# One grid for all slots, and another order of work at the entry of both FFNs of a hybrid mLSTM and attention trunk

## The chip, the cores and the metric

The kernel runs on one core of one Trainium2 chip. The metric is the device time of one execution in microseconds: the median of three runs of the kernel before is 2521.12 us (2517.9 to 2522.45). All times below are of the kernel before.

## The reference

Input x is 1024 rows of 1024 float32 numbers. Two layers follow one another; each adds a mixer and an FFN to the residual stream, with a norm before and after each (rmsnorm of rows of 1024). Layer 0's mixer is a chunkwise mLSTM with 8 heads, layer 1's a causal attention with forget gates and 16 heads on keys and values that are projected once. What matters here is the FFN, which stands in both layers:

```python
def conv_ffn(h, w_up, conv_w, conv_b, w_down):      # h 1024x1024, w_up 1024x5632
    u = h @ w_up
    up = jnp.pad(u, ((0, 0), (CONV_WIDTH - 1, 0), (0, 0)))
    y = conv_b
    for j in range(CONV_WIDTH):                       # 3 taps along the rows
        y = y + conv_w[j] * up[:, j:j + S]
    gate, val = jnp.split(y, 2, axis=-1)              # 2816 columns each
    return (jax.nn.gelu(gate, approximate=True) * val) @ w_down
```

## The kernel before

**Products.** Every float32 operand of a large product is split into a high and a low part (`split`, L197: ScalarE casts the high part, L199, VectorE subtracts it, L200), and each product is three matmuls: high with high, high with low, low with high. The up product works on column tiles of 128 columns of the gate half and the same 128 of the value half: 22 column tiles in each FFN. A column tile is a 2x2 block product by Strassen and Winograd: seven products named 11, 12, S2, S1, S3, S4 and 22, in that order, each of 12 matmuls of 128x512 (L815), so 84 matmuls for a column tile. Products 11 and 12 run after one another into two banks of PSUM, and so on; a tile's results are copied or added out of the banks by ScalarE (L824) and VectorE (L822). After S4 the value half goes through the convolution of three taps (L831, L833), after 22 the gate half and the Gelu (L848); every second column tile `keep` (L857) forms sums on GpSimd and sends seven pieces to DRAM. The down product (L976) reads them back, in matmuls of the same shape with both operands in the tile x.

**Weights of a column tile.** SyncE loads the raw weights of a tile into slots 8 and 9 (even tiles) or 10 and 11 (odd). `prep_up` makes the stationary operands: 11 goes to slot 18, 12 to slot 0, S2 and S1 (from sums that GpSimd forms in a slot `tmp`, L789 to L792) to slots 1 and 2, S3 and 22 to slots 3 and 4, S4 to slot 5. In the steady state a product of tile f is followed by `prep_up` of the same product of tile f+1, into the same slots.

**The moving operand.** The rows of the normalised residual stream, transposed and split, are the moving operand. Products 11, 12, S3 and 22 read them from x (a tile of 16384 numbers per partition); S2, S1 and S4 read sums of row tiles from the pair slots p0 to p5.

**Slots.** The arena is a set of slots, each one tag of a tile pool with 128 partitions: 1024 numbers wide (4096 bytes), 1088 for slots 0, 1, 15, 27, 29 and 30 (4352 bytes), 1032 for slots 2 and 31 (4128 bytes), and 2048 for p0, p3, p2, p4, p1 and p5 (two slots each, 8192 bytes). They lie behind one another in memory in the order 10, 5, p1, 16, 15, 0, 27, 29, 1, 30, 11, 31, then 8, 18, p0, 7, 3, p3, 6, p4, p2, 4, 2, then 14, p5, 9, 32; x and the identity stand in a second pool. Since 4096, 4352 and 8192 are multiples of 128 and 4128 is 32 more than one, the slots of the second group begin 32 bytes further on a 128-byte line than the first group, and those of the third 64 bytes further. x begins where the third group begins.

**The entry of an FFN.** `out_stage` computes the mixer's output product for eight row tiles, adds it to the residual stream (`tail_a`: Square, scale, L215, L216), normalises the result (`tail_b`, L225), forms sums of two row tiles (`sums`, L730 to L733) and transposes each piece on TensorE with a split into x or a pair slot (`turns`: four transposes of L207, one cast L199, one subtraction L200 a turn). TensorE's instructions stand in source order there (`in_order`). For the last row tiles, `lead` begins the column tiles: products 11 and 12 of tiles 0 and 1, then product 11 of tile 2 with the turns of the last row tile in between, then product 12 of tile 2; `run` goes on with the other five products of tile 0, of tile 1, of tile 2, and then tile after tile. ScalarE and VectorE are ordered by the scheduler.

Of the kernel before, what the change touches and what calls it, by code (L numbers as in the profile page):

```python
# [34 lines left out]
SLACK = 0, 20  # L35
PIECES = {5: (8, 20, 26, 32, 38), 10: (6, 8, 17, 21, 25, 29, 33, 37, 41, 45)}

WIDE = {0: 1088, 1: 1088, 15: 1088, 27: 1088, 29: 1088, 30: 1088, 2: 1032, 31: 1032}
PAIRS = (19, 22), (20, 21), (23, 24), (25, 12), (26, 13), (28, 17)
PAIR = {i: (j, n) for j, two in enumerate(PAIRS) for n, i in enumerate(two)}  # L40
BLOCK = {(0, 0): 0, (0, 1): 1, (1, 1): 2, (1, 0): 3}
# [1 line left out]
ORDER = (0, 4, 1, 5, 2, 6, 3, 7)  # L43
# [5 lines left out]
PRODUCTS = ("11", "12", "S2", "S1", "S3", "S4", "22")  # L49


class Core:
# [30 lines left out]
    def slot(self, i, dt):  # L83
# [3 lines left out]
        if self.slots.get(key, (None, None))[1] != dt:  # L87
            n, name = (WIDE.get(i, 1024), key) if half is None else (2048, f"p{key}")
            self.slots[key] = self.arena.tile([P, n], dt, tag=name, name=name), dt
# [258 lines left out]
def mlstm(k, x, gpre, w_in, b_gate, hnorm, w_out, gpost, gnext, scr, x1, params, follow):  # L348
# [338 lines left out]
    with k.in_order():  # L687
        out_stage(arena, w, None, x, x1, gpost, gnext, follow, ((), (4, 5), (2, 3)), turns=late)


class Ffn:
# [34 lines left out]
    def sums(self, h0, h1):  # L726

        tt = self.nc.vector.tensor_tensor
        (s1, s2), (s3, s4) = ((self.k.f(i)[:, :512], self.k.f(i)[:, 512:]) for i in (31, 27))
        tt(s1, h1[:, :512], h1[:, 512:], ALU.add)  # L730
        tt(s2, s1, h0[:, :512], ALU.subtract)
        tt(s3, h0[:, :512], h1[:, :512], ALU.subtract)
        tt(s4, h0[:, 512:], s2, ALU.subtract)  # L733
# [38 lines left out]
    def prep_up(self, f, name):  # L772

        k, nc = self.k, self.nc
        if f >= self.NF:
            return
        b11, b12, b21, b22 = self.raw(f)
        tmp = k.f(6 if f else self.tmp)
        t2, t1 = tmp[:, :512], tmp[:, 512:]

        def split(name, src, n=512):
            k.split(self.right(name, 0, n), self.right(name, 1, n), src)

        if name == "11":
            split("11", b11)
        elif name == "12":
            split("21", b21)
        elif name == "S2":
            nc.gpsimd.tensor_tensor(t1, b12, b11, ALU.subtract)  # L789
            nc.gpsimd.tensor_tensor(t2, b22, t1, ALU.subtract)  # L790
            nc.gpsimd.tensor_tensor(b12, b22, b12, ALU.subtract)
            nc.gpsimd.tensor_tensor(b21, b21, t2, ALU.subtract)  # L792
        elif name == "S1":
            split("T2", tmp, 1024)
        elif name == "S4":
            split("22", b22)
        elif name == "22":
            split("T3", k.f((9, 11)[f % 2]), 1024)
# [73 lines left out]
        tt(a12, a12, s2, ALU.subtract)  # L872
        nc.sync.dma_start(self.act[5, p], a12)

    def begin(self, tmp):

        self.tmp = tmp
        self.load_up(0)
        self.load_up(1)
        for name in PRODUCTS[:3]:  # L880
            self.prep_up(0, name)

    def lead(self, turns):

        self.steps_up(0, PRODUCTS[:2])
        self.steps_up(1, PRODUCTS[:2], False)
        for name in PRODUCTS[3:]:
            self.prep_up(0, name)
        self.load_up(2)
        for name in PRODUCTS[:2]:  # L890
            self.prep_up(2, name)
        meanwhile = self.up(2, PRODUCTS[0])
        next(meanwhile)
        for _ in turns:
            next(meanwhile, None)
        for _ in meanwhile:
            pass
        self.steps_up(2, PRODUCTS[1:2], False)

# [88 lines left out]
    def run(self):  # L990

        k, nc, ng = self.k, self.nc, self.NG
        rest = PRODUCTS[2:]
        self.steps_up(0, rest)
        self.load_up(3)
        for name in PRODUCTS[:2]:
            self.prep_up(3, name)
        self.steps_up(1, rest)
        self.load_up(4)
        self.steps_up(2, rest)  # L1000
        for f in range(3, self.NF):
            if f + 2 < self.NF:
                self.load_up(f + 2)
            if f < self.NF - 1:
                self.steps_up(f, PRODUCTS)
        todo = {"": [("", 0), ("11", 0), ("", 1), ("11", 1), ("", 2), ("11", 2)], "S2": [("11", 3), ("11", 4), ("11", 5)],
                "S1": [("21", 0), ("21", 1), ("21", 2)]}
        later = [[("21", 3), ("12", 0)], [("21", 4), ("12", 1)], [("21", 5), ("12", 2)]]
        later += [[("12", g)] for g in (3, 4, 5)] + [[("22", g)] for g in range(ng)]
        for name in ("",) + PRODUCTS:  # L1010
            if name:
                self.steps_up(self.NF - 1, (name,))
            for w, g in todo.get(name, ()):
                self.load_right(w, g) if w else self.load_left(g)
        self.prep_down(0)
        self.prep_down(1)
        self.last()
        end = 7 * ng
        for q in range(end - 3):
            i, g = divmod(q, ng)  # L1020
            self.prep_down(q + 2)
            for w, g_ in later[q] if q < len(later) else ():
                self.load_right(w, g_)
            for m in range(4):
                self.down(q, m)
                if g == ng - 1:
                    self.read(i, m)
            if i == 6:
                self.tails(g)
        self.prep_down(end - 1)  # L1030
        for m in range(4):
            for q in range(end - 3, end):
                self.down(q, m)
            self.ends(m)
        if self.follow is None:
            return
        self.third(7)
        k.tail_c(self.y(0), 0, (2, 3))
        for t in range(NT):
            if t < NT - 1:  # L1040
                k.tail_c(self.y(t + 1), t + 1, ((0, 1), (2, 3))[t % 2])
            next(self.follow)
# [57 lines left out]
def out_stage(k, w, gather, src, dst, gpost, gnext, f, ys, begun=0, turns=iter(())):  # L1100

    nc = k.nc
    gpb, gnb = k.f(6), k.f(7)
    k.bcast_row(gpb, gpost)
    k.bcast_row(gnb, gnext)

    def y_of(n):
        return k.wide(*ys[n % 3])

    def z_of(n):  # L1110
        return k.f((32, 15)[n % 2])

    for n, t in enumerate(ORDER):
        res = k.f(29 if gather else (29, 30)[n % 2])
        nc.sync.dma_start(res, src[t * P:(t + 1) * P])
        y = y_of(n)
        if n > 1:
            turns = f.turns(z_of(n), ORDER[n - 2])
        for i, _ in enumerate(k.out_steps(y, t, w, begun if n == 0 else 0, 8)):
            if i == 23 if n == 0 else i > 7 and i % 3 == 0:  # L1120
                next(turns, None)
        if gather and n + 2 < NT:
            gather(n + 2)
        if n == NT - 1:
            f.begin(30 if gather else 29)
        k.tail_a(z_of(n), y, res, t, gpb, dst)
        k.tail_b(z_of(n), res, gnb)
        if n % 2:
            f.sums(z_of(n - 1), z_of(n))
    for _ in f.turns(z_of(6), ORDER[6]):  # L1130
        pass
    f.lead(f.turns(z_of(7), ORDER[7], (1, -1)))
    f.run()


def fox(k, kv_w, kv_b, w_qg, w_out, kv_norm, gpre, gpost, gnext, scr, src, dst, follow):
# [140 lines left out]
    def steps(jobs):  # L1277


        ahead = jobs[0][1]()  # L1280
        yield
        for n, (name, load_, run) in enumerate(jobs):
            w = ahead
            later = []
            ahead = jobs[n + 1][1](later) if n + 1 < len(jobs) else None
            places = PIECES[len(later)] if later else ()
            for i, _ in enumerate(run(w)):
                piece = i in places
                if piece:
                    later.pop(0)()  # L1290
                yield name, i + 1, piece
# [196 lines left out]
    with k.in_order():  # L1488
# [71 lines left out]
        gather(1)  # L1560
        out_weights(3)
        out_stage(arena, w, gather, src, dst, gpost, gnext, follow, ((4, 5), (), (2, 3)), 5)


# [64 lines left out]
```

## Time and profile before

| what | us |
|---|---|
| median of the runs | 2521.12 |
| profiled execution | 2521.05 |
| its span, first to last instruction | 2519.3 |
| TensorE busy | 2453.5 |
| VectorE busy | 1562.0 |
| ScalarE busy | 1166.3 |
| GpSimd busy | 640.4 |

The span is cut into stages by TensorE's work: the mLSTM and its projections, FFN0 from about 476 us, the attention layer, FFN1 from about 1845 us. On the timeline a row is a run of equal instructions: start, busy time, engine, line, operation, out<-in (s is any slot, p a pair slot, x the tile x, b and two are banks of PSUM), shape, and in brackets the idle time before it and what ended it. The start of one row and of the next give the distance of matmuls; the busy time of a row of n matmuls has the length of one, about 0.39 us, in place of the last distance.

### The profile page before, as it was taken

How to read it: one execution, taken by the hardware profiler on the slowest of the kernel's cores; microseconds unless marked ns; L12 is line 12 of the kernel's file. 1: busy time of each engine (PE TensorE's matmuls, PEld its weight loads, DVE VectorE, ACT ScalarE, POOL GpSimd, SP SyncE). 2: the span in 40 equal slices, each digit the busy share in tenths (PEclk: the TensorE clock that was granted, in tenths of full speed). 3: DMA queues.
4: the chain of work that ended last, by engine and by line, in shares of the span. 5: the costliest groups of instructions: out<-in, count | busy, mean ns of one | idle time of the engine just before them, and what ended most of it. 6: DMA issues, size and time to landing. Idle time of an engine off the chain costs nothing.

```text
span 2519.3 us, 34088 instructions
## 1 busy us (share of the span) xinstructions
PE 2453.5 (97%) x12552; PEld 2044.2 (81%) x12552; DVE 1562.0 (62%) x2442; ACT 1166.3 (46%) x2078; POOL 640.4 (25%) x545
## 2 busy tenths in 40 slices
PE   8999999899999999999999999999989999999998
PEld 7988998778888888888878888887877888888886
DVE  6312666666667678467555565556667666667746
ACT  5212454444454454455455455555435444545344
POOL 0000110134553520002223333232023544442000
PEclk9999999999999999999999999999999999999999
DMA  7444442322332365444654454553333322337443
GB/s 222 129 125 137 114 128 92 105 76 96 100 108 93 106 226 194 126 142 138 200 154 129 143 147 138 147 155 117 101 98 95 110 96 97 109 100 279 136 136 127
DMA packets 291795, 332.04 MB, mean 132 GB/s; under 512 B 21036, under 2 KB 208268, under 8 KB 291628
## 3 DMA queue, kind: packets, MB, share of 16 engines
q1 hardware_dynamic: 291052, 328.82, 42.1%
q8 instruction: 98, 1.61, 0.3%
q10 hardware_dynamic: 576, 1.05, 0.1%
q14 instruction: 69, 0.57, 0.1%
HBM read 230.03 MB, written 99.78 MB: 131 GB/s over the span
## 4 chain that ended last, share of the span: by engine, by line
PE 87%; DVE 5%; DMA 3%; ACT 3%; issue 1%; POOL 1%; SPq 0%; DVEq 0%; ACTq 0%; POOLq 0%
PE b L815 32%; PE b L976 11%; PE b L1210 11%; PE b L288 4%; PE b L307 4%; PE two L976 3%; PE b L1389 3%; PE two L396 3%; PE two L307 2%; PE b L1377 2%; PE two L288 2%; PE two L1362 2%; PE b L1226 2%; PE b L207 1%; PE b L1362 1%
## 5 line engine op out<-in xcount | busy, mean ns | idle before, releaser
L815 PE MATMUL b<-x,s 128*128 128x512 f32 x2112 | 512.6, 397 | 9.7 <-ACT x L199 4.6
L815 PEld LDWEIGHTS b<-x,s 128*128 128x128 f32 x2112 | 398.5, 189 | 106.6 <-ACT x L199 5.2
L199 ACT CAST s<-s 128x1024 fp32r<-128x1024 f32 (+3 forms) x319 | 230.5, 728 | 405.8 <-PE b L815 339.6
L200 DVE TENSOR_TENSOR s<-s,s 128x512 fp32r<-128x512 f32 (+3 forms) x312 | 280.9, 904 | 205.0 <-ACT s L199 199.8
L815 PE MATMUL b<-p,s 128*128 128x512 f32 x1584 | 385.7, 397 | 8.8 <-ACT s L824 8.8
L815 PEld LDWEIGHTS b<-p,s 128*128 128x128 f32 x1584 | 299.1, 189 | 81.5 <-ACT s L824 10.5
L976 PE MATMUL b<-x 128*128 128x512 f32 x1452 | 336.1, 389 | 1.5 <-DVE x L200 1.5
L976 PEld LDWEIGHTS b<-x 128*128 128x128 f32 x1452 | 272.4, 188 | 59.1 <-DVE x L200 2.4
L833 DVE SCALAR_TENSOR_TENSOR s<-s,cp,s 128x1023 f32<-128x1023 f32 (+1 forms) x176 | 241.8, 1374 | 31.2 <-ACT s L831 29.5
L1210 PE MATMUL b<-x,s 128*128 128x512 f32 x816 | 239.7, 411 | 1.0 <-DVE F L1174 1.0
L199 ACT CAST x<-s 128x1024 fp32r<-128x1024 f32 (+2 forms) x144 | 128.6, 918 | 229.8 <-PE b L976 178.2
L200 DVE TENSOR_TENSOR x<-s,x 128x1024 fp32r<-128x1024 f32 (+2 forms) x144 | 153.6, 1088 | 117.6 <-ACT x L199 115.8
L1369 POOL TENSOR_SCALAR p<-p,ring 128x256 f32<-128x256 f32 (+7 forms) x128 | 99.5, 780 | 322.7 <-DVE ring L1368 311.6
L792 POOL TENSOR_TENSOR s<-s,s 128x512 f32<-128x512 f32 x44 | 94.8, 2154 | 331.9 <-issue 219.8
L1210 PEld LDWEIGHTS b<-x,s 128*128 128x128 f32 x816 | 148.3, 190 | 25.6 <-DVE F L1174 1.2
L822 DVE TENSOR_TENSOR s<-s,b 128x512 f32<-128x512 f32 x132 | 90.5, 685 | 117.0 <-PE b L815 117.0
L789 POOL TENSOR_TENSOR s<-s,s 128x512 f32<-128x512 f32 x44 | 57.9, 1315 | 314.9 <-DMA s<-in_ffn_w_up_dram 188.5
L200 DVE TENSOR_TENSOR p<-b,p 128x384 fp32r<-128x384 f32 (+1 forms) x166 | 94.2, 584 | 51.0 <-ACT p L199 50.4
L831 ACT ACTIVATE s<-s,cp 128x1024 f32<-128x1024 f32 x88 | 109.6, 1246 | 34.8 <-DVE s L822 14.2
L199 ACT CAST p<-b 128x512 fp32r<-128x512 f32 (+2 forms) x182 | 90.5, 513 | 73.7 <-PE b L1377 45.0
L824 ACT COPY s<-b 128x512 f32<-128x512 f32 x176 | 102.3, 581 | 38.2 <-PE b L815 37.8
L1210 PE MATMUL b<-x,p 128*128 128x512 f32 x336 | 105.7, 416 | 0.0
(294 smaller groups left out, 3990.2 us busy)
## 6 DMA issues: line engine op xcount, KB each, us to landing
s<-in_ffn_w_up_dram SPq DMA_DIRECT2D x176, 256.0 KB, 3.3
s<-act SPq DMA_DIRECT2D x70, 512.0 KB, 4.0
act<-s SPq DMA_DIRECT2D x110, 256.0 KB, 2.1
s<-in_mlstm_w_in_dram SPq DMA_DIRECT2D x24, 512.0 KB, 6.1
act<-s SPq DMA_DIRECT2D x22, 512.0 KB, 2.8
s<-in_ffn_w_down_dram SPq DMA_DIRECT2D x20, 512.0 KB, 5.4
p<-in_ffn_w_down_dram SPq DMA_DIRECT2D x20, 512.0 KB, 8.1
x<-s SPq DMA_DIRECT2D x19, 512.0 KB, 2.6
```

What stands on the lines that cost most here:

```text
L199: self.nc.scalar.copy(hi, src)
L200: self.nc.vector.tensor_tensor(lo, src, hi, ALU.subtract)
L288: self.nc.tensor.matmul(out, st, mv, start=i == 0, stop=i == n - 1)
L307: self.nc.tensor.matmul(self.at(ps, c), st, mv[:, c:c + 512], start=kk == 0 and st is sh and mv is wh, stop=kk == 7 and st is sl)
L792: nc.gpsimd.tensor_tensor(b21, b21, t2, ALU.subtract)
L815: nc.tensor.matmul(out, w[a][:, d], mv, start=first and d == 0 and i == 0, stop=d == 3 and i == 2, skip_group_check=True)
L824: nc.scalar.copy(out, bank)
L831: nc.scalar.activation(y, u, AF.Identity, bias=cp[:, 3, col:col + 1], scale=cp[:, 2, col:col + 1])
L833: nc.vector.scalar_tensor_tensor(y[:, j:], u[:, :S - j], cp[:, 2 - j, col:col + 1], y[:, j:], ALU.mult, ALU.add)
L976: self.nc.tensor.matmul(self.banks(i)[m], st[:, p, cs], mv[:, p], start=i in (0, 1, 3) and g == p == e == 0, stop=g == self.NG - 1 and p = ...
L1210: nc.tensor.matmul(ps, st[d], k.xs(mv, d, c, 512), start=d == 0 and i == 0, stop=d == ND - 1 and i == 2)
L1369: nc.gpsimd.tensor_scalar(pt[:, :n], pt[:, :n], rd, 1.0, ALU.mult, ALU.mult)
```

## The change

The change has two parts. First, slots 2 and 31 become 1088 numbers wide (4352 bytes). All slots, x and the identity then begin at the same place of a 128-byte line. Second, the entry of both FFNs is written in another order. The last row tile's `tail_a`, `tail_b` and `sums` move into `lead`, between the first products; product 11 and 12 of tiles 0 and 1 come first, then each turn of the last row tile is followed by one product of tile 0 (S2, S1, S3, S4, 22), and tile 2's products 11 and 12 move into the ordinary loop. ScalarE and VectorE follow the source order in this part too (`manual_schedule`). The weight sums of tile 1 use slot 32 instead of slot 6.

```diff
--- before.py
+++ after.py
@@ -35,7 +35,7 @@
 SLACK = 0, 20
 PIECES = {5: (8, 20, 26, 32, 38), 10: (6, 8, 17, 21, 25, 29, 33, 37, 41, 45)}
 
-WIDE = {0: 1088, 1: 1088, 15: 1088, 27: 1088, 29: 1088, 30: 1088, 2: 1032, 31: 1032}
+WIDE = {0: 1088, 1: 1088, 15: 1088, 27: 1088, 29: 1088, 30: 1088, 2: 1088, 31: 1088}
 PAIRS = (19, 22), (20, 21), (23, 24), (25, 12), (26, 13), (28, 17)
 PAIR = {i: (j, n) for j, two in enumerate(PAIRS) for n, i in enumerate(two)}
 BLOCK = {(0, 0): 0, (0, 1): 1, (1, 1): 2, (1, 0): 3}
@@ -775,7 +775,7 @@
         if f >= self.NF:
             return
         b11, b12, b21, b22 = self.raw(f)
-        tmp = k.f(6 if f else self.tmp)
+        tmp = k.f((self.tmp + (6,))[min(f, 2)])
         t2, t1 = tmp[:, :512], tmp[:, 512:]
 
         def split(name, src, n=512):
@@ -872,7 +872,7 @@
         tt(a12, a12, s2, ALU.subtract)
         nc.sync.dma_start(self.act[5, p], a12)
 
-    def begin(self, tmp):
+    def begin(self, *tmp):
 
         self.tmp = tmp
         self.load_up(0)
@@ -880,22 +880,24 @@
         for name in PRODUCTS[:3]:
             self.prep_up(0, name)
 
-    def lead(self, turns):
-
-        self.steps_up(0, PRODUCTS[:2])
+    def lead(self, turns, tail, sums):
+
+
+        self.steps_up(0, PRODUCTS[:1])
+        tail()
+        self.steps_up(0, PRODUCTS[1:2])
+        sums()
+        self.prep_up(0, "S1")
         self.steps_up(1, PRODUCTS[:2], False)
-        for name in PRODUCTS[3:]:
-            self.prep_up(0, name)
+        next(turns)
+        self.prep_up(0, "S4")
+        self.prep_up(0, "22")
         self.load_up(2)
+        for name in PRODUCTS[2:]:
+            next(turns, None)
+            self.steps_up(0, (name,))
         for name in PRODUCTS[:2]:
             self.prep_up(2, name)
-        meanwhile = self.up(2, PRODUCTS[0])
-        next(meanwhile)
-        for _ in turns:
-            next(meanwhile, None)
-        for _ in meanwhile:
-            pass
-        self.steps_up(2, PRODUCTS[1:2], False)
 
 
 
@@ -990,15 +992,9 @@
     def run(self):
 
         k, nc, ng = self.k, self.nc, self.NG
-        rest = PRODUCTS[2:]
-        self.steps_up(0, rest)
         self.load_up(3)
-        for name in PRODUCTS[:2]:
-            self.prep_up(3, name)
-        self.steps_up(1, rest)
-        self.load_up(4)
-        self.steps_up(2, rest)
-        for f in range(3, self.NF):
+        self.steps_up(1, PRODUCTS[2:])
+        for f in range(2, self.NF):
             if f + 2 < self.NF:
                 self.load_up(f + 2)
             if f < self.NF - 1:
@@ -1122,14 +1118,17 @@
         if gather and n + 2 < NT:
             gather(n + 2)
         if n == NT - 1:
-            f.begin(30 if gather else 29)
+            break
         k.tail_a(z_of(n), y, res, t, gpb, dst)
         k.tail_b(z_of(n), res, gnb)
         if n % 2:
             f.sums(z_of(n - 1), z_of(n))
-    for _ in f.turns(z_of(6), ORDER[6]):
-        pass
-    f.lead(f.turns(z_of(7), ORDER[7], (1, -1)))
+    f.begin(30 if gather else 29, 32)
+    with k.tc.manual_schedule(engines={mybir.EngineType.Activation, mybir.EngineType.DVE}):
+        for _ in f.turns(z_of(6), ORDER[6]):
+            pass
+        k.tail_a(z_of(7), y, res, t, gpb, dst)
+        f.lead(f.turns(z_of(7), ORDER[7]), partial(k.tail_b, z_of(7), res, gnb), partial(f.sums, z_of(6), z_of(7)))
     f.run()
```

On ScalarE, at FFN0's entry, the row of the casts into x (x_78), with the weight splits (s5, s1, s3) and the Squares (junk) of the last row tile, before:

```order
L199 CAST p4_555<-b1_85 128x4x128
L199 CAST s5_3298<-s8_4185 128x512
L199 CAST s1_137<-s29_136 128x1024
L199 CAST x_78<-b0_84 128x4x128
L199 CAST s3_3505<-s9_4186 128x1024
L176 ACTIVATE junk_81,ring_82<-b4_88 128x512
L176 ACTIVATE junk_81,ring_82<-b5_89 128x512
L199 CAST x_78<-b1_85 128x4x128
L199 CAST x_78<-b0_84 128x4x128
```

And now:

```order
L199 CAST p4_555<-b1_85 128x4x128
L199 CAST x_78<-b0_84 128x4x128
L199 CAST x_78<-b1_85 128x4x128
L199 CAST x_78<-b0_84 128x4x128
L176 ACTIVATE junk_81,ring_82<-b4_88 128x512
L176 ACTIVATE junk_81,ring_82<-b5_89 128x512
L190 ACTIVATE ring_82<-ring_82,eps_79 128x1
L824 COPY s14_4243<-b2_86 128x512
L199 CAST s18_1829<-s10_4191 128x512
```

The casts into s5, s1 and s3 no longer stand between the casts into x; the Squares follow the last cast into x.

On TensorE, in `lead` of FFN0, behind products 11 and 12 of tile 0 (banks b2 and b3): the turns (from s31, s27 and s15, into banks two and b1), before:

```order
L815 MATMUL b4_88<-x_78,s18_1829 128x512 x12
L815 MATMUL b5_89<-x_78,s0_130 128x512 x12
L815 MATMUL b0_84<-x_78,s18_1829 128x512 x3
L207 MATMUL two_83<-ident_66,s31_156 128x128 x4
L815 MATMUL b0_84<-x_78,s18_1829 128x512 x3
L207 MATMUL b1_85<-ident_66,s31_156 128x128 x4
L815 MATMUL b0_84<-x_78,s18_1829 128x512 x3
L207 MATMUL two_83<-ident_66,s27_3333 128x128 x4
L815 MATMUL b0_84<-x_78,s18_1829 128x512 x3
L207 MATMUL b1_85<-ident_66,s27_3333 128x128 x4
L207 MATMUL two_83<-ident_66,s15_129 128x128 x4
L815 MATMUL b1_85<-x_78,s0_130 128x512 x12
```

And now, where p2, p3, s1 and s2 are the operands of product S2 of tile 0:

```order
L815 MATMUL b4_88<-x_78,s18_1829 128x512 x12
L815 MATMUL b5_89<-x_78,s0_130 128x512 x12
L207 MATMUL b1_85<-ident_66,s31_156 128x128 x4
L207 MATMUL b0_84<-ident_66,s31_156 128x128 x4
L815 MATMUL b2_86<-p2_3766,s1_137 128x512
L815 MATMUL b2_86<-p3_550,s1_137 128x512
L815 MATMUL b2_86<-p2_3766,s2_3504 128x512
L815 MATMUL b2_86<-p2_3766,s1_137 128x512
L815 MATMUL b2_86<-p3_550,s1_137 128x512
L815 MATMUL b2_86<-p2_3766,s2_3504 128x512
L815 MATMUL b2_86<-p2_3766,s1_137 128x512
L815 MATMUL b2_86<-p3_550,s1_137 128x512
```

The 24 matmuls of tile 2 (banks b0 and b1) have gone from here; two turns stand between tile 1's products and S2 of tile 0, and the third, from s27, stands behind S2.

## Rows read from the trace of the kernel before

**Rows 1.** The page, part 1: busy us (share of the span) x instructions.

```profile
PE 2453.5 (97%) x12552; PEld 2044.2 (81%) x12552; DVE 1562.0 (62%) x2442; ACT 1166.3 (46%) x2078; POOL 640.4 (25%) x545
```

**Rows 2.** PE timeline of one column tile: start us, busy us, instructions [idle before].

```profile
603.54 5.75 PE L815 MATMUL b<-p,s 128*128 128x512 f32 x24
609.13 2.96 PE L815 MATMUL b<-x,s 128*128 128x512 f32 x12
611.93 2.94 PE L815 MATMUL b<-p,s 128*128 128x512 f32 x12
614.70 8.49 PE L815 MATMUL b<-x,s 128*128 128x512 f32 x36
623.03 5.75 PE L815 MATMUL b<-p,s 128*128 128x512 f32 x24
```

**Rows 3.** PE timeline in FFN0's down product.

```profile
1022.94 2.88 PE L976 MATMUL b<-x 128*128 128x512 f32 x12
1025.66 2.88 PE L976 MATMUL two<-x 128*128 128x512 f32 x12
```

**Rows 4.** PE timeline, matmuls of L288, weights in pair slots, then in other slots.

```profile
122.50 5.76 PE L288 MATMUL two<-x,p 128*128 128x512 f32 x24
128.10 5.76 PE L288 MATMUL b<-x,p 128*128 128x512 f32 x24
...
175.90 5.66 PE L288 MATMUL two<-x,s 128*128 128x512 f32 x24
```

**Rows 5.** PE timeline at FFN0's entry.

```profile
482.16 1.12 PE L207 MATMUL b<-ident,s 128*128 128x128 f32 x4 [3.46 <-DVE x L200]
...
487.04 10.69 PE L815 MATMUL b<-x,s 128*128 128x512 f32 x37 [0.84 <-DVE x L200]
...
510.56 5.75 PE L815 MATMUL b<-p,s 128*128 128x512 f32 x24
...
534.58 3.06 PE L815 MATMUL b<-p,s 128*128 128x512 f32 x12 [1.52 <-ACT s L824]
...
562.84 7.39 PE L815 MATMUL b<-p,s 128*128 128x512 f32 x24 [2.90 <-ACT s L824]
```

**Rows 6.** PE timeline at FFN1's entry.

```profile
1850.20 0.66 PE L207 MATMUL b<-ident,s 128*128 128x128 f32 x4 [2.27 <-DVE x L200]
...
1930.61 7.40 PE L815 MATMUL b<-p,s 128*128 128x512 f32 x24 [2.87 <-ACT s L824]
```

**Rows 7.** Windows: us, busy of each engine, PEclk, DMA share, GB/s.

```profile
481.00:491.00 10.00, 5.87 (x14) 4.16 (x15) 8.33 (x13) 3.37 (x8) 5.42 (x4) 0.50 0.28 80
```

**Rows 8.** PE timeline, 256-wide matmuls of L288, moving operand in slots.

```profile
92.32 0.40 PE L288 MATMUL b<-s,x 128*128 128x256 f32 x2
92.56 0.28 PE L288 MATMUL b<-p,x 128*128 128x256 f32 x1
92.68 0.40 PE L288 MATMUL b<-s,x 128*128 128x256 f32 x2
...
108.90 5.60 PE L288 MATMUL b<-s,x 128*128 128x256 f32 x48
114.34 2.88 PE L288 MATMUL two<-s,x 128*128 128x256 f32 x24
```

**Rows 9.** ACT timeline at FFN0's entry.

```profile
479.20 1.04 ACT L199 CAST s<-s 128x1024 fp32r<-128x1024 f32 x1 [1.89 <-POOL s L790]
...
482.66 1.04 ACT L199 CAST s<-s 128x1024 fp32r<-128x1024 f32 x1 [1.93 <-POOL s L792]
483.61 0.59 ACT L176 ACTIVATE junk<-b 128x512 bf16<-128x512 f32 x1
```

**Rows 10.** DVE timeline at FFN0's entry.

```profile
489.08 2.27 DVE L216 SCALAR_TENSOR_TENSOR s<-s,ring,s 128x1024 f32<-128x1024 f32 x1
...
494.46 1.28 DVE L225 SCALAR_TENSOR_TENSOR s<-s,ring,s 128x1024 f32<-128x1024 f32 x1
```

**Rows 11.** POOL timeline at FFN0's entry.

```profile
488.99 1.28 POOL L791 TENSOR_TENSOR s<-s,s 128x512 f32<-128x512 f32 x1
```

**Rows 12.** ACT timeline in column tile 2 of FFN0.

```profile
558.52 1.25 ACT L831 ACTIVATE s<-s,cp 128x1024 f32<-128x1024 f32 x1 [6.48 <-DMA act<-s]
```

## The prediction

> **What bounds the kernel now.** I read the engine shares first. TensorE is busy 97% of the span [rows 1], so the 44 column tiles of the two FFN up products (84 matmuls each) set the time, and only two kinds of thing can help: a shorter matmul, or less idle time between matmuls. So I read next, on TensorE's timeline, how far apart equal matmuls start, and then where TensorE waits.
>
> For the first kind take one steady column tile. Its products start at 603.54, 609.13, 611.93, 614.70 and 623.03 us, and the last two rows are one period of 19.49 us apart [rows 2]: S2 and S1 together 5.59 us for 24 matmuls (233 ns each), S3 2.80 for 12, S4 2.77 for 12, then 36 (22, 11, 12) in 8.33. A full period is 84 matmuls in 19.49 us, 232.0 ns each. The down product has matmuls of the very same shape, with both operands in the tile x; there 12 start every 2.72 us, 226.7 ns each [rows 3]. Both stand in stretches where TensorE waits for nothing. What differs is where the operands lie. The stationary operand of the first lies in slots 18, 0, 1 to 5, that of the second in x, and by the slots' widths slot 18 and slots 2 to 4 begin 32 bytes off x's place in a 128-byte line, slots 0, 1 and 5 64 bytes off it. The third row group repeats the test inside one line of code, with x moving: weights in a pair slot 32 bytes off, 24 matmuls in 5.60 us (233.3 ns); in slots that lie 64 bytes off, 5.66 us of busy time where the other has 5.76, so 0.10 us less over 23 intervals, 229.0 ns [rows 4]. I read from this that a 512-wide matmul takes 226.7 ns when its two operands lie alike, 229.0 at 64 bytes' difference and 233.3 at 32.
>
> For the second kind: at FFN0's entry the second matmul of the first column tile starts at 487.04, and its product S2 only at 510.56; TensorE waits 3.46 us before the transposes at 482.16, 1.52 at 534.58 and 2.90 at 562.84 [rows 5]. FFN1's entry has the same waits, 2.27 us at 1850.20 and 2.87 at 1930.61 [rows 6]. Between 481 and 491 us the granted clock stood at 0.50 [rows 7], the level of 1.2 GHz, behind the waits.
>
> **The grid.** Slots 2 and 31 grow from 4128 to 4352 bytes; every slot then starts at the same place of a 128-byte line, and so does x. No instruction is added. At 226.7 ns a column tile of 84 takes 19.04 us instead of 19.49: 0.45 us x 44 = -19.8 us. L1210 (1152 matmuls, x moving against weights in slots of all kinds) gains between 2.3 ns [229.0 to 226.7] and 6.6 ns [233.3]; I take the middle, 4.4 ns: -5.0 us. Of L288's 512-wide matmuls the 224 with weights in pair slots gain 6.6 ns: -1.5. L307 (768, slots moving, x stationary) I put at half of that, 2.9 ns: -2.2. The down product does not change its operands' place. Against this stand the 256-wide matmuls, which behave otherwise: with slot operands lying like x, three start every 0.36 us (120.0 ns), while with slots 64 bytes off 48 start every 5.44 us (113.3 ns) [rows 8]. On one grid all 1920 of them would be of the first kind. Their price lies between 0 (they follow the 512-wide rule after all) and 6.7 ns x 1920 = +12.9 us; I count 6.7 ns for the 384 that now lie 64 bytes off (+2.6) and 1.5 ns for the rest, which lie 32 off (+2.3), and 1.1 for the 272-wide ones: +6.0. Together -19.8 - 5.0 - 1.5 - 2.2 + 6.0 = -22.5 us. The bounds: were it the stationary operand's own place that counts and not its distance from the moving one, all would run at 229.0, L815 would gain 84 x 3.0 ns x 44 = 11.1, the down product would lose 1848 x 2.3 ns = 4.3, and with the 256-wide at their worst nothing or -5 would be left; if the 256-wide lose nothing and L1210 gains fully, -32.
>
> What the Trainium skill says speaks against this term. Its page "TensorE: Matmul & The Clock Gate" (Part 2, "Step-by-step: what each phase is for") has two independent read ports, one for the streaming operand and one for the weights, and says that loading the next tile's weights "doesn't steal SBUF read bandwidth from the running matmul". By that rule the place of the weights cannot matter and this term would be 0, not -22.5; the 233.3 and 229.0 ns of one line, with the same moving tile, do not fit it.
>
> **The entry.** ScalarE at FFN0's entry does the weight split of slot 5 at 479.20, after waiting 1.89 us for GpSimd's L790 to write what it reads, and that of slot 1 at 482.66, after 1.93 us for L792 [rows 9]. Behind them in its queue stand the casts of x that TensorE waits for, and behind the second also two Squares of 0.59. The new order puts the casts first. What goes is 1.89 + 1.04 + 1.93 + 1.04 = 5.9 us and those two Squares, 7.1; a little comes back, since VectorE's low halves then follow one another, so I take 6.9: second matmul at 480.1. From there VectorE carries the chain, with the same instructions as now: low halves of x to 481.4, z (two L215) to 483, the res update L216 to 485.5 (2.27 us now, beside GpSimd's L791 of 1.28 us at 488.99; the like L225 takes 1.28 alone [rows 10, 11]), one split, Square and norm to 488.2, L225 to 489.5, then L822, one split and four half-width sums of 0.6 us to 493.1, transposes and a split (2.3 us): S2's second matmul at 495.6, where it is at 510.79 now (510.56 + 0.23). That is 15.2 us earlier. But it is a change of order: 24 matmuls of tile 2 (5.55 us at 231 ns) that used to lie in this stretch and three of the transposes' turns (1.7) come later, so 15.2 - 5.55 - 1.7 = 7.9 us is saved.
>
> What becomes late next: S1's weights. GpSimd's L792 for tile 0 and the splits of slots 1 to 4 now run beside VectorE's chain, which is denser; if L216-like pairs collide (2.27 against 1.28) S1 waits between 0 and 1.75 us. I take 0.9. Tile 1's S4 waits already 1.52 us for the copy L824, which stands behind a cast, a table load and a Gelu; with a 0.6 us split more ahead of it, +0.5. And tile 2's stall goes: 2.90 us at 562.84, where ScalarE's activation had waited 6.48 us for a transfer out of the slot that it writes [rows 12]. The new order puts tile 2's S4 five products later, so the transfer has 5 x 2.8 us more; with the stall goes the lower clock after it (the 24 matmuls at 562.84 are busy 7.39 us, where those at 510.56 are 5.75: 1.6), together -4.5. FFN0: -7.9 + 0.9 + 0.5 - 4.5 = -11.0. At FFN1 the first wait is 2.27 instead of 3.46, so 1.2 less is to be had: -9.8. The entry's sum is -20.8; bounds: -5, if a wait in VectorE's order takes the 7.9 of both entries back, to -25, if S1 and S4 do not wait.
>
> I count nothing for the clock in the first 48 matmuls: at the higher level they are done at 491.3, before S2 can start at 495.6, so up to 4 us lost to the lower one there would be hidden.
>
> On the 0.9 us: "SBUF — State Buffer" in the Trainium skill ("Who interferes with whom") says that a VectorE instruction with two SBUF inputs contends with a GpSimd instruction that reads SBUF. The 2.27 us of L216 agrees; by the rule applied to all of GpSimd's work there, S1 would wait the whole 1.75 and the entries give 19 instead of 20.8.
>
> **Sum.** The profiled execution took 2521.05 us (its span 2519.3 and 1.75 around it), 0.1 us under the median shown, 2521.12, so no correction is needed: 2521.05 - 22.5 - 20.8 = 2477.7, I say 2478.
>
> **Rivals.**
> (a) The place of the operands does nothing; the 226.7 ns belongs to the down product for another reason (it alternates between banks, its weights are re-used). For it: the skill's rule above. Against it: the two rates inside L288 [rows 4]. Time: 2521 - 20.8 = 2500.
> (b) The entry's order gives nothing: ScalarE and VectorE in source order put one late input ahead of ready work, and the stall moves from x's casts to S2 or S1. For it: 7.9 us rests on a chain of some fifteen VectorE instructions, and with GpSimd beside it each can take 2.27 for 1.28. Time: 2521 - 22.5 = 2498.5.
> (c) Operands that lie alike at the start of a 128-byte line do better than 226.7 (now all such pairs lie at 64), as the 113.3 ns of the 256-wide show to be possible: 3 ns on 7848 matmuls more, 2455.
> (d) Slower: lying alike becomes the bad case for 512-wide too, as it is for 256-wide [rows 8]. Then all 7848 512-wide matmuls run at 233.3: the down product +1848 x 6.6 = 12.2, L815 (19.60 - 19.49) x 44 = +4.8, L1210 +2.5, the rest +1.5, 256- and 272-wide +6: +27, and with the entry's -20.8 the time is 2527. It decides once the mean interval rises by more than 20.8 us / 7848 = 2.7 ns. Against it: the down product, whose operands lie alike at 64 bytes, is the fastest [rows 3].
>
> **Chances.** The forecast 0.66, with its own range 2464 to 2492; (a) 0.10, (b) 0.13, (c) 0.06, (d) 0.05. For eight in ten I take 2463 to 2504, which leaves out (c), (d) and the tails. A measurement of this kernel tells about 0.2%, 5 us, from no change; faster by more than that hold the forecast and (a) to (c) but for tails, 0.93; within it 0.04; slower 0.03, from (d).
>
> **What will show it.** In a steady column tile a period of 19.0 us instead of 19.49 and 12 matmuls in 2.72; 256-wide matmuls at 120 instead of 113.3; the down product unchanged. At FFN0's entry no weight split ahead of the casts of x, the second matmul near 480, S2 near 495.6 after two column tiles' 11 and 12, no wait of 2.9 us in tile 2. I am wrong if the period stays at 19.49, if the down product's 2.72 changes, or if S2 starts after 500.

## The result

The changed kernel takes 2475.26 us (median of four runs, 2472.1 to 2477.49), the kernel before 2521.51 beside it: ratio 0.9814, 95% interval 0.9802 to 0.9826. That is 46 us less; 2478 was forecast. The profiled execution has a span of 2474.8 us.

TensorE's busy share rises from 97 to 98%, its busy time falls by 29.4 us against [rows 1]:

```profile
PE 2424.1 (98%) x12552; PEld 2041.3 (82%) x12552; DVE 1551.5 (63%) x2442; ACT 1162.6 (47%) x2078; POOL 658.3 (27%) x545
```

The steady column tile, TensorE's timeline of the kernel after (start us, busy us, instructions, in brackets the idle time before):

```profile
600.68 8.32 PE L815 MATMUL b<-x,s 128*128 128x512 f32 x36
608.84 5.60 PE L815 MATMUL b<-p,s 128*128 128x512 f32 x24
614.28 2.88 PE L815 MATMUL b<-x,s 128*128 128x512 f32 x12
...
619.72 8.32 PE L815 MATMUL b<-x,s 128*128 128x512 f32 x36
```

The first and last row are one period apart, 19.04 us where [rows 2] have 19.49. All seven products now run at one rate, 2.72 us for 12: S2 and S1 5.44 for 24, S3 and S4 likewise (614.28 to 619.72), and 36 in 8.16. The down product, which answers to [rows 3], has not moved, and the 256-wide matmuls that took 113.3 ns in [rows 8] now take 5.76 us for 48, 120.0 ns:

```profile
110.81 5.92 PE L288 MATMUL b<-s,x 128*128 128x256 f32 x48
116.57 3.04 PE L288 MATMUL two<-s,x 128*128 128x256 f32 x24
...
1004.46 2.88 PE L978 MATMUL two<-x 128*128 128x512 f32 x12
1007.18 2.88 PE L978 MATMUL b<-x 128*128 128x512 f32 x12
```

TensorE's timeline at FFN0's entry, against [rows 5], and then at the same place of FFN1:

```profile
481.42 8.68 PE L815 MATMUL b<-x,s 128*128 128x512 f32 x37 [0.23 <-DVE x L200]
...
490.97 2.57 PE L815 MATMUL b<-x,s 128*128 128x512 f32 x10 [0.88 <-DVE s L200]
...
495.84 2.78 PE L815 MATMUL b<-p,s 128*128 128x512 f32 x11 [0.69 <-DVE p L200]
...
521.48 3.01 PE L815 MATMUL b<-p,s 128*128 128x512 f32 x12 [2.13 <-ACT s L824]
...
551.53 5.78 PE L815 MATMUL b<-p,s 128*128 128x512 f32 x24
...
1864.30 4.61 PE L815 MATMUL b<-p,s 128*128 128x512 f32 x12 [2.13 <-ACT s L824]
1868.75 8.33 PE L815 MATMUL b<-x,s 128*128 128x512 f32 x36
```

The second matmul starts at 481.42 instead of 487.04, and the run of 37 is busy 8.68 us instead of 10.69. S2's second matmul starts at 495.84 instead of 510.79. The wait of 2.90 us in the fourth column tile is gone (551.53 has none). Tile 1's S4 waits longer than before, 2.13 us against 1.52, and at FFN1 its 12 matmuls then take 4.45 us (1864.30 to 1868.75) instead of 2.72. The windows show the lower clock there, and that FFN0's entry no longer falls to it, where [rows 7] had 0.50 (PEclk, the mean granted clock of the window, is the third number from the end). The fall at FFN1 does not belong to every execution: behind the same wait of 2.13 us the 12 matmuls take 2.85 us at FFN0 here, and 2.85 at FFN1 in a second profile of the same kernel (after_again, 1863.82 to 1866.67).

```profile
481.00:491.00 10.00, 8.89 (x39) 6.90 (x38) 8.26 (x19) 6.39 (x14) 1.48 (x2) 1.00 0.20 73
1864.00:1869.00 5.00, 4.70 (x14) 3.70 (x15) 3.00 (x5) 0.53 (x2) 3.69 (x3) 0.66 0.32 105
```

ScalarE's timeline at FFN0's entry shows the casts of x ahead of the Squares with no weight split between, where [rows 9] had two; further on, what stands between the end of tile 1's S1 (516.47) and the copy that its S4 needs:

```profile
478.68 0.59 ACT L199 CAST x<-b 128x512 fp32r<-128x512 f32 x1 [1.24 <-PE b L207]
480.05 1.28 ACT L199 CAST x<-b 128x512 fp32r<-128x512 f32 x2 [0.78 <-PE b L207]
481.22 0.60 ACT L176 ACTIVATE junk<-b 128x512 bf16<-128x512 f32 x1
...
516.49 1.05 ACT L199 CAST s<-s 128x1024 fp32r<-128x1024 f32 x1 [1.96 <-PE b L815]
517.57 1.28 ACT L848 ACT_TABLE_LOAD   x1
518.86 1.06 ACT L848 ACTIVATE s<-s 128x1024 f32<-128x1024 f32 x1
...
520.85 0.58 ACT L824 COPY s<-b 128x512 f32<-128x512 f32 x1
```

From the starts of the same matmuls in both traces, the 44.5 us between the two spans (2519.3 and 2474.8) come from here, up to rounding:

| where | forecast | measured |
|---|---|---|
| L815's matmuls, 44 column tiles | -19.8 | -19.6 (16.1 in 36 tiles, 8 x 0.44) |
| layer 0's mixer, to the last matmul of L307 | with the next row | +1.3 |
| the layer between the FFNs | -2.7 together | -3.4 |
| entry of FFN0, to the end of the fourth column tile | -11.0 | -12.7 |
| entry of FFN1, likewise | -9.8 | -10.2 |
| behind FFN1's down product | 0 | +0.2 |

The entries are what is left of these stretches (101.3 us before and 86.9 after at FFN0, 99.9 and 87.9 at FFN1) after 4 x 0.44 us of shorter matmuls are taken off; they begin with the last run of L307's matmuls. The rows of the mixer and of the layer between are not much larger than what profiles of one grid differ by: the last matmul of L307 in layer 0 starts between 477.9 and 480.8 us on the old one (before, source_order_only, entry_only) and between 478.5 and 480.6 on the new one, and from the first down product to the last L307 of the second layer it is 701.3 to 705.0 us on the old, 697.8 to 701.6 on the new.

### The profile page after: what moved, and what is told of

Read it like the earlier page. It is cut to its first block, busy times and chain, and to the rows that moved or that the text cites. A ratio compares the mean times of both kernels' runs of the same rounds, so it can differ in the third digit from the quotient of the medians.

```text
span 2474.8 us, 34098 instructions
## 1 busy us (share of the span) xinstructions
PE 2424.1 (98%) x12552; PEld 2041.3 (82%) x12552; DVE 1551.5 (63%) x2442; ACT 1162.6 (47%) x2078; POOL 658.3 (27%) x545
## 4 chain that ended last, share of the span: by engine, by line
PE 89%; DVE 5%; ACT 2%; DMA 2%; issue 1%; POOL 0%; SPq 0%; DVEq 0%; ACTq 0%; POOLq 0%
PE b L815 33%; PE b L978 11%; PE b L1209 10%; PE b L288 4%; PE b L307 4%; PE two L978 3%; PE two L307 3%; PE two L396 3%; PE b L1388 3%; PE b L1376 2%; PE two L288 2%; PE b L1225 2%; PE two L1361 2%; PE b L207 1%; DVE x L200 1%
## 5 line engine op out<-in xcount | busy, mean ns | idle before, releaser
L815 PE MATMUL b<-x,s 128*128 128x512 f32 x2112 | 495.0, 389 | 1.8 <-DVE s L200 1.3
L815 PEld LDWEIGHTS b<-x,s 128*128 128x128 f32 x2112 | 396.0, 188 | 85.7 <-DVE s L200 2.1
L200 DVE TENSOR_TENSOR s<-s,s 128x512 fp32r<-128x512 f32 (+3 forms) x312 | 269.1, 867 | 188.7 <-ACT s L199 183.6
L815 PE MATMUL b<-p,s 128*128 128x512 f32 x1584 | 377.8, 391 | 6.1 <-ACT s L824 4.3
L815 PEld LDWEIGHTS b<-p,s 128*128 128x128 f32 x1584 | 297.0, 188 | 71.6 <-ACT s L824 5.1
L1209 PE MATMUL b<-x,s 128*128 128x512 f32 x816 | 238.4, 409 | 0.9 <-DVE F L1173 0.9
L200 DVE TENSOR_TENSOR x<-s,x 128x1024 fp32r<-128x1024 f32 (+2 forms) x144 | 153.6, 1088 | 117.0 <-ACT x L199 116.2
L822 DVE TENSOR_TENSOR s<-s,b 128x512 f32<-128x512 f32 x132 | 90.3, 684 | 99.5 <-PE b L815 99.5
L789 POOL TENSOR_TENSOR s<-s,s 128x512 f32<-128x512 f32 x44 | 58.7, 1335 | 277.6 <-DMA s<-in_ffn_w_up_dram 189.6
L200 DVE TENSOR_TENSOR p<-b,p 128x512 fp32r<-128x512 f32 x168 | 95.4, 584 | 48.5 <-ACT p L199 48.0
```

The source lines that it names most:

```text
L200: self.nc.vector.tensor_tensor(lo, src, hi, ALU.subtract)
L815: nc.tensor.matmul(out, w[a][:, d], mv, start=first and d == 0 and i == 0, stop=d == 3 and i == 2, skip_group_check=True)
L1209: nc.tensor.matmul(ps, st[d], k.xs(mv, d, c, 512), start=d == 0 and i == 0, stop=d == ND - 1 and i == 2)
```

## The experiments

Theory T: a 512-wide matmul's interval depends on how far apart its two operands begin on a 128-byte line, and the entry's gain is the order of work; the two add up. The rivals: the place does nothing; the entry's order does nothing, or only one half of it matters.

### Each part alone

**grid_only**: the kernel before with one line changed.

```diff
-WIDE = {..., 2: 1032, 31: 1032}
+WIDE = {..., 2: 1088, 31: 1088}
```

> The kernel before with slots 2 and 31 at 4352 bytes and nothing else changed. Theory (a 512-wide matmul takes 226.7 ns when its two operands begin at the same place of a 128-byte line): period of a steady column tile 19.04 us instead of 19.49, 44 times -0.45 = -19.7, the other stages -2.3 as the trace after shows them, so 2521.5 - 22 = 2499.5; the waits at the entries stay as before (3.5, 1.5 and 2.9 us at FFN0). Rival (the place does nothing, the new order did it all): 2521. Rival (the two parts lean on one another, shorter matmuls uncover the entry's waits): 2503 to 2510, with waits at the entries longer than before.

Measured: 2499.79 us, ratio 0.9916 (0.9902 to 0.9929). TensorE's timeline has the short period (19.04 us between the last two rows), and the stall in the fourth tile is still there, 3.42 us against 2.90 in [rows 5]:

```profile
563.48 7.44 PE L815 MATMUL b<-p,s 128*128 128x512 f32 x24 [3.42 <-ACT s L824]
...
614.32 8.32 PE L815 MATMUL b<-x,s 128*128 128x512 f32 x36
...
633.36 6.96 PE L815 MATMUL b<-x,s 128*128 128x512 f32 x30
```

**entry_only**: the changed kernel with the old widths.

```diff
-WIDE = {..., 2: 1088, 31: 1088}
+WIDE = {..., 2: 1032, 31: 1032}
```

> The changed kernel with slots 2 and 31 back at 4128 bytes, so only the entry's new order is left. Theory: -12.7 us at FFN0 and -10.1 at FFN1 as in the trace after, 2521.5 - 22.8 = 2498.7, and a steady period of 19.49. Rival (the parts lean on one another): the two single gains add up to less than 40 or more than 50 of the 46 us. If the place of the operands were all, 2521.

Measured: 2494.87 us, ratio 0.9900 (0.9884 to 0.9915), with the long period:

```profile
605.94 8.49 PE L815 MATMUL b<-x,s 128*128 128x512 f32 x36
...
625.43 8.49 PE L815 MATMUL b<-x,s 128*128 128x512 f32 x36
```

The two gains, 20.9 and 25.8 us beside their own runs of before (17.9 to 24.7 and 21.4 to 29.2 by the intervals), add up to 46.7, where the whole change gave 46.3. So the parts are independent within what the runs can tell, and neither "the place does nothing" (2521 for the first) nor "the order does nothing" (2521 for the second) holds.

### Which half of the entry

**no_source_order**: the new order of products, ScalarE and VectorE ordered by the scheduler.

```diff
-    with k.tc.manual_schedule(engines={mybir.EngineType.Activation, mybir.EngineType.DVE}):
-        for _ in f.turns(z_of(6), ORDER[6]):
+    for _ in f.turns(z_of(6), ORDER[6]):
...
```

> The changed kernel without the source order on ScalarE and VectorE at the entry (the scheduler orders them); TensorE's order is the new one. ScalarE then has the weight splits of slots 5, 1 and 3 ahead of the casts of x again. Theory: the second matmul of FFN0 goes back from 481.4 to about 487 and S2 from 495.8 to about 501, +5.5 us at each entry, while the stall of 2.9 us in the fourth column tile stays away: 2475.3 + 11 = 2486. Rival (the order of products alone makes the gain, since S2's start hangs on VectorE): within 3 us of 2475. Rival (the gain is all from the source order): 2498.

Measured: 2484.94 us, ratio 0.9861 (0.9847 to 0.9874), 9.7 above the changed kernel. ScalarE waits for GpSimd ahead of the casts of x just as in [rows 9] (1.90 us, and 1.93 before the next weight split at 483.21), the second matmul starts at 486.17, S2's second at 503.03, and no stall follows in the fourth tile:

```profile
479.75 1.04 ACT L199 CAST s<-s 128x1024 fp32r<-128x1024 f32 x1 [1.90 <-POOL s L790]
```

```profile
486.17 13.72 PE L815 MATMUL b<-x,s 128*128 128x512 f32 x47 [0.58 <-DVE x L200]
...
503.03 2.80 PE L815 MATMUL b<-p,s 128*128 128x512 f32 x11 [1.53 <-DVE p L200]
```

**source_order_only**: the old order of products, with the source order on ScalarE and VectorE.

```diff
-    for _ in f.turns(z_of(6), ORDER[6]):
-        pass
-    f.lead(f.turns(z_of(7), ORDER[7], (1, -1)))
+    with k.tc.manual_schedule(engines={mybir.EngineType.Activation, mybir.EngineType.DVE}):
+        for _ in f.turns(z_of(6), ORDER[6]):
+            pass
+        f.lead(f.turns(z_of(7), ORDER[7], (1, -1)))
```

> The kernel before with the source order on ScalarE and VectorE for the turns of the last two row tiles and the first products, TensorE's order and the slots as before. Theory: the casts of x come first, second matmul at about 481 instead of 487, S2 at about 505 instead of 510.6, the 2.9 us stall stays: -5.5 at each entry, 2510. Rival (source order delays the weight splits so that S2 or the later products wait instead): 2521 or more.

Measured: 2523.5 us, ratio 1.0014 (1.0005 to 1.0022): the rival was right and T's 2510 wrong. The second matmul does start at 481.91. But S2 starts at 512.00, later than before:

```profile
481.91 5.57 PE L815 MATMUL b<-x,s 128*128 128x512 f32 x23 [1.32 <-DVE x L200]
...
501.04 0.50 PE L815 MATMUL b<-x,s 128*128 128x512 f32 x1 [3.85 <-DVE s L200]
...
512.00 5.75 PE L815 MATMUL b<-p,s 128*128 128x512 f32 x24
```

```profile
503.87 0.62 ACT L199 CAST s<-s 128x512 fp32r<-128x512 f32 x1 [7.77 <-DMA s<-in_ffn_w_up_dram]
```

Two late inputs eat the gain. The matmul at 501.04 is the third of tile 2's product 11; it waits 3.85 us for its low weights, which VectorE makes only after the low halves of three other splits. And the source puts tile 2's weight split for product 12 before the turns: its raw weights land so late that ScalarE waits 7.77 us for the DMA, and the casts of the turns stand behind it. In the new order tile 2's splits come last. So the halves of the entry are not a sum: source order alone is worth nothing, the order of products alone (with slot 32) about 16 us (25.8 less 9.7), and both together 25.8.

**sums_slot6**: tile 1's weight sums in slot 6, as before.

```diff
-    f.begin(30 if gather else 29, 32)
+    f.begin(30 if gather else 29, 6)
```

> The changed kernel with the weight sums of column tile 1 in slot 6 again, as before, instead of slot 32. Slot 6 holds the row that tail_a of the last row tile still reads, slot 32 the rows that the sums read until 493 us. Theory: the sums of tile 1 are not needed before its product S2, some 15 us later, so the slot makes no difference: within 3 us of 2475.3. Rival (GpSimd starts earlier with slot 6 and lies beside VectorE's chain): the L216 and L225 of the last row tile take 2.3 us instead of 1.28 and S2 starts 1 to 2 us later at each entry, +2 to +4.

Measured: 2481.6 us, ratio 0.9849 (0.9834 to 0.9864), 6.3 above the changed kernel. T was wrong, the rival's mechanism right and its size too small (and L225, which it named too, stays at 1.28). VectorE's, GpSimd's and TensorE's timeline of this run:

```profile
485.15 2.42 DVE L216 SCALAR_TENSOR_TENSOR s<-s,ring,s 128x1024 f32<-128x1024 f32 x1
487.48 1.75 DVE L200 TENSOR_TENSOR s<-s,s 128x512 fp32r<-128x512 f32 x1
```

```profile
485.19 1.29 POOL L789 TENSOR_TENSOR s<-s,s 128x512 f32<-128x512 f32 x1 [2.29 <-DVE s L215]
486.56 2.12 POOL L790 TENSOR_TENSOR s<-s,s 128x512 f32<-128x512 f32 x1
```

```profile
499.00 2.83 PE L815 MATMUL b<-p,s 128*128 128x512 f32 x11 [1.63 <-DVE p L200]
```

L216 and L789 of the changed kernel:

```profile
484.89 1.28 DVE L216 SCALAR_TENSOR_TENSOR s<-s,ring,s 128x1024 f32<-128x1024 f32 x1
```

```profile
493.58 2.14 POOL L789 TENSOR_TENSOR s<-s,s 128x512 f32<-128x512 f32 x1 [11.11 <-PE b L815]
```

With slot 6 GpSimd starts tile 1's sums at 485.19, beside L216, which then takes 2.42 us instead of 1.28, and the split behind it 1.75 us, where the next like one takes 0.68; S2's second matmul comes at 499.00 instead of 495.84; counted from the last matmul of the mixer it is 2.9 us later, and 3.0 at FFN1. Slot 32 holds rows that the sums on VectorE read until 493.45, so it keeps GpSimd waiting until the chain is through (the row names a matmul of L815 that ends at 493.54, just behind them). A wait for a slot is here worth 6 us. The section "Who interferes with whom" of the Trainium skill's page "SBUF — State Buffer" has a VectorE instruction with two SBUF inputs contend with a GpSimd instruction that reads SBUF; these rows agree.

### Where the operands lie

**slot31_only**: one of the two pads, so that slots 14, 9, 32, p5 and x begin 32 bytes off all others.

```diff
-WIDE = {..., 2: 1088, 31: 1088}
+WIDE = {..., 2: 1032, 31: 1088}
```

> The changed kernel with slot 2 back at 4128 bytes, slot 31 still at 4352: slots 14, 9, 32, pair slot p5 and x begin 32 bytes off all other slots. Theory (only the distance of the two operands' starts counts): products with x moving and weights in slots go back to 2.79 us for 12 (11, 12, S3, 22), S2 and S1 stay at 2.72 although their operands are the same slots that took 2.79 before, S4 lies between (its low part is in p5, 4 of 12 matmuls); period 4 x 2.79 + 2 x 2.72 + 2.74 = 19.34 instead of 19.05, 44 x 0.29 = +12.8; L1209 and L307 up to +5 more: 2488 to 2493. The down product stays at 2.72. Rival (a slot's own place counts, not the distance): all seven products stay at 2.72 except S4, and the down product with x now 32 bytes off slows to 2.79, +1848 x 6 ns = 11. Rival (one pad is enough): 2475.

Measured: 2497.38 us, ratio 0.9917 (0.9903 to 0.9932), outside T's 2488 to 2493. TensorE's timeline:

```profile
600.41 2.96 PE L815 MATMUL b<-p,s 128*128 128x512 f32 x12
603.21 8.56 PE L815 MATMUL b<-x,s 128*128 128x512 f32 x36
611.61 5.64 PE L815 MATMUL b<-p,s 128*128 128x512 f32 x24
617.09 2.97 PE L815 MATMUL b<-x,s 128*128 128x512 f32 x12
```

The products with x moving are back at 2.80 us for 12 (36 in 8.40), and S2 with S1, in the very slots that took 5.59 us in [rows 2], need 5.48. The down product, with x on another place of the line than in any other kernel here, lasts 212.71 us from its first matmul to its last at FFN0, against 212.73 before. So it is the distance and not the slot's own place. But the size is beyond T: S4 takes 2.80, though only every third of its matmuls has an operand in p5, and the period is 19.48 instead of 19.34. The 256-wide matmuls take 118.3 ns here, at 32 bytes (48 in 5.68 us, 109.99 to 115.67).

**x_64**: x moved by 64 bytes against all slots.

```diff
+        self.gap = c.tile([P, 16], F32, name="gap")
+        nc.gpsimd.memset(self.gap, 0.0)
         self.x = c.tile([P, 16384], F32R, name="x")
```

> The changed kernel with x moved by 64 bytes (a small tile ahead of it), the slots as they are. Theory of the distance: 512-wide matmuls with x against slots take 229.0 ns: 11, 12, S3 and 22 2.75 us for 12, S2, S1, S4 and the down product stay at 2.72: period 19.16 instead of 19.05, +4.9; L1209, L307 and L288 +2 to +4; the 256-wide matmuls of L288 and L396 go from 120.0 to 113.3 ns, up to -12.9 if all stand on the path, but in the attention of layer 0 they lie beside other waits, so -5 to -10: 2470 to 2480. Rival (own place counts): the down product goes to 2.75 us for 12, +4.

Measured: 2484.12 us, ratio 0.9859 (0.9844 to 0.9874), 8.9 above the changed kernel and outside T's 2470 to 2480. The 256-wide matmuls came back to 113.3 ns as expected (48 in 5.44, first two rows), the column tile did not:

```profile
110.49 5.60 PE L290 MATMUL b<-s,x 128*128 128x256 f32 x48
115.93 2.88 PE L290 MATMUL two<-s,x 128*128 128x256 f32 x24
...
607.80 5.65 PE L817 MATMUL b<-p,s 128*128 128x512 f32 x24
613.29 2.93 PE L817 MATMUL b<-x,s 128*128 128x512 f32 x12
616.06 2.93 PE L817 MATMUL b<-p,s 128*128 128x512 f32 x12
618.83 8.42 PE L817 MATMUL b<-x,s 128*128 128x512 f32 x36
627.08 5.75 PE L817 MATMUL b<-p,s 128*128 128x512 f32 x24
```

The period is 19.28 us (607.80 to 627.08; every second one is 19.39), where 19.16 was expected. S4, all of whose operands lie alike, takes 2.77 us between S3 and 22, which lie 64 bytes apart, and S2 with S1 5.49 instead of 5.44. Matmul by matmul in this trace, S2's 12 intervals after product 12 are 234, 231, 233, 236, 224, 231, 236, 228, 232, 231, 227 and 226 ns (medians over 44 tiles), and S1's, right behind, all 227. So behind a product whose operands lie apart it takes some ten matmuls before the interval settles (eight in slot31_only). This is not a matter of distance alone: in sums_slot6, where all operands lie alike, the intervals behind the wait of 1.67 us at 489.29 are 340, 240, 235, 234, 236, 224, 231, 235, 229, 232 and 231 ns, almost the same run. It accounts for the period of x_64, where mixed places cost more than the mean of their distances. It does not account for S4 in slot31_only, whose last six intervals still average 233 ns: there one operand in three is enough.

### The wait that grew

**gelu_late**: tile 0's Gelu and its product with the value half move behind product S1 of tile 1 (`gated` holds these two instructions).

```diff
             for _ in self.up(f, name):
                 pass
+            if f == 1 and name == "S1":
+                self.later()
...
                 g = self.conv(f, 0)
-                nc.scalar.activation(g, g, AF.Gelu_apprx_tanh)
-                nc.vector.tensor_tensor(g, g, self.value, ALU.mult)
+                self.later = partial(self.gated, g, self.value)
+                if f:
+                    self.later()
...
```

> The changed kernel with the Gelu of column tile 0 (and its product with the value half) issued behind product S1 of tile 1 and its copy, so that the table load of 1.28 us and the Gelu of 1.06 no longer stand ahead of the copy that tile 1's S4 waits for. Theory: the wait of 2.13 us before tile 1's S4 goes at both entries, and with it the lower clock behind it at FFN1 (12 matmuls in 4.45 us instead of 2.72, 1.7 us): 2475.3 - 2 x 2.1 - 1.7 = 2469.4. Rival (the copy is late for another reason, the casts ahead of it): 2474 or more, and the wait shrinks by less than 1 us.

Measured: 2468.84 us, ratio 0.9801 (0.9785 to 0.9818). ScalarE and TensorE around tile 1's S4, at FFN0 and FFN1:

```profile
517.29 0.57 ACT L824 COPY s<-b 128x512 f32<-128x512 f32 x1
517.88 1.28 ACT L862 ACT_TABLE_LOAD   x1
```

```profile
519.02 2.88 PE L815 MATMUL b<-p,s 128*128 128x512 f32 x12
...
1857.51 2.88 PE L815 MATMUL b<-p,s 128*128 128x512 f32 x12
1860.23 8.32 PE L815 MATMUL b<-x,s 128*128 128x512 f32 x36
```

The copy ends at 517.9, the table load and the Gelu follow it, and S4 follows S3 without a wait; at FFN1 its 12 matmuls take 2.72 us. A wait of 0.70 us for VectorE's L822 comes up in the fourth tile instead, which lasts 20.03 us against 19.21. To compare it with the changed kernel on one chip, both ran once more.

> The changed kernel once more, beside the version with the late Gelu on one chip. All theories: 2475, 45 to 47 us under the kernel before.

> The version with tile 0's Gelu behind tile 1's S1, on the same chip as the changed kernel. Theory: 5 to 7 us under it (two waits of 2.1 us, and the lower clock behind one of them). Rival (the first difference came from two chips): within 2 us of it.

Measured: 2475.31 us for the changed kernel (ratio 0.9822, 0.9809 to 0.9835) and 2470.58 for this version (0.9804, 0.9791 to 0.9817): 4.7 us less, a little under T's 5 to 7; the times of the two do not overlap (2472.58 to 2476.27 and 2468.2 to 2472.14). In these two profiles, neither of which falls to the lower clock at S4, the entries account for 3.2 us (1.6 each: the wait of 2.13 gone, some of it back in the fourth tile), so the rest of the 4.7 is not traced to this edit.

## Why the prediction was right, and where not

**The grid.** Right in mechanism and size: the period 19.04 as forecast, -22.5 forecast for the whole grid and 20.9 measured alone. Two terms under it were off and partly made up for each other, which was luck. L1210's -5.0 was too large: where two of its matmuls follow one another without a wait (676 pairs in each trace under 300 ns) they start 230.5 ns apart on the mean instead of 232.8, so 2.3 ns and not 4.4, and the stretch from its first matmul to its last lasts 551.9 us instead of 553.7. They stand there between other matmuls, so few reach a settled interval; that this is the reason is not shown. The 256-wide term of +6.0 (with the 272-wide) was too large as well; layer 0's mixer is +2.6 at its worst point, of which L307 gives back 1.3, and 1.2 of it stand before 41 us, where entry_only with the old widths has 1.3 too.

**The entry's chain.** S2 was to start its second matmul at 495.6 and does at 495.84, with layer 0's mixer ending 1.3 us later than assumed. So the chain itself is 1.1 us shorter than worked out. The step that was mis-sized is L216's 2.27 us: it takes 1.28. The prediction gave slot 32 no effect; it keeps GpSimd away, and sums_slot6 prices that at 6 us. For the same reason the 0.9 us for S1's weights did not come: no wait stands before S1. With these two the entries' 20.8 came out too small: the traces show 22.9, and entry_only 25.8, beyond the bound of 25. So the forecast gain, 43.3 us, was 3 us short of the 46.3 measured, with the grid's term 1.6 us too large and the entries' 2 to 5 too small; that the two missed in opposite ways was luck.

**S4 and the stall.** Tile 1's S4 waits 0.6 us more, 0.5 was forecast; not forecast were the 1.7 us of lower clock behind this wait at FFN1. In after_again, without them, FFN1's entry gives 11.7 instead of 10.2. The fourth tile takes 19.21 us instead of 24.21; 0.44 of it is the grid, so 4.55 for the stall against 4.5 forecast. I named the place wrongly: the matmul that waits at 562.84 is S2 of the fourth tile, behind tile 2's activation, not S4 of tile 2. And tile 2's S4 moves back by two products behind tile 1's last, 11 and 12 of tile 2 (5.4 us), not by five; that was enough, for ScalarE's activation now starts at 544.34 with no wait for the transfer.

**The clock.** The first 37 matmuls now run at the granted 1.00. That this alone buys nothing, as forecast, agrees with the rows but has no run of its own: TensorE is through early and waits for VectorE, 0.88 us at 490.97 and 0.69 at 495.84.

**The rivals.** (a) fell with grid_only; what the prediction quoted of the Trainium skill's "TensorE: Matmul & The Clock Gate" (Part 2, "Step-by-step: what each phase is for"), that the next weights' load takes no read bandwidth from the running matmul, does not cover it: the same matmuls take 226.7 to 233.3 ns by where the weights lie. (b) fell for the change, but source_order_only shows its mechanism at work in the old order of products. (c) and (d) fell: matmuls whose operands lie alike take 226.7 ns at 64 bytes as at 0, and at 32 in slot31_only.

What stays open is why the interval depends on the distance at all, why 256-wide matmuls prefer 64 bytes and 512-wide none, why S4 pays in full for one operand in three, and what carries over from one product to the next; no run here looks inside.

## What to carry to other kernels

When the same matmul runs at two rates in one trace, compare where its operands begin before looking for a wait: two slots 224 bytes wider were worth 21 us here. An order by hand on one engine pays only if every input it puts first is early; read which DMA or GpSimd result each moved instruction needs. And a copy that frees a bank belongs ahead of a table load and an activation that nobody waits for.

## What the runs showed of the hardware that was not expected

- The interval of 512-wide matmuls has a memory: with all operands alike, S2 takes 2.77 us instead of 2.72 when the product before it had operands 64 bytes apart, and settles only in its last two matmuls. A wait does the same with all operands alike (sums_slot6 behind 489.29: 240 ns at first, still 231 ten matmuls later).
- One operand in three 32 bytes off costs as much as all: S4 in slot31_only, 2.80 us for 12, still 233 ns a matmul at its end.
- The 256-wide matmuls go the other way, 113.3 ns at 64 bytes (before, x_64), 118.3 at 32 (slot31_only) and 120.0 at none (before, after).
- GpSimd's subtractions beside VectorE's L216 took it from 1.28 to 2.42 us. The one that began with it, L789, kept its 1.29; the next, L790, which lies beside the end of L216 and a split, took 2.12 instead of 1.29.
